# Last projection panel's context products beside the first neighbourhood jobs, and a layer norm's square sums joined ahead of the matrix engine

## The chip, the cores and the metric

The kernel runs on one core of a Trainium2 chip. The metric is the device time of one execution in microseconds (us); less is better. The core's engines work beside each other and wait for each other through semaphores: TensorE (PE, with its weight loads PEld), VectorE (DVE), ScalarE (ACT), GpSimd (POOL) and SyncE (SP), which here only issues transfers (DMAs). Each engine, and each DMA queue, works through its instructions in a fixed order.

## The reference

Two layers of a diffusion backbone over 512 latent tokens and 256 context tokens, width 1024, all in float32. What matters here:

```python
for l in range(DEPTH):                                   # 2 layers
    sh_a, sc_a, g_a, sh_f, sc_f, g_f = jnp.split(silu_c @ mod_w[l] + mod_b[l], 6, axis=-1)
    csh_a, csc_a, cg_a, csh_f, csc_f, cg_f = jnp.split(silu_cc @ mod_w[l] + mod_b[l], 6, axis=-1)
    a_lat = modulate(h_lat, sh_a, sc_a)                  # rms_norm(x) * (1 + scale) + shift
    a_ctx = modulate(h_ctx, csh_a, csc_a)
    # layer 0: p = a @ w_in; multi-head latent heads and 2-D neighbourhood heads; @ w_out
    # layer 1: sliding-window attention with grouped queries; @ w_out
    h_lat = h_lat + g_a * o_lat
    h_lat = h_lat + g_f * swiglu(modulate(h_lat, sh_f, sc_f), w_gate_up[l], w_down[l])
    # the context tokens likewise in layer 0
return rms_norm(h_lat, final_norm)
```

`rms_norm` divides each token by the root of the mean of its squared features. The six modulation vectors per layer and stream are products of a 1024-vector with a 1024 x 6144 matrix.

## The kernel before, in words

Features lie on the 128 partitions, tokens along the free dimension: a stream of width 1024 is eight tiles (k or m = 0 to 7) of 128 x 768, the first 512 columns latent (`LATS`), the last 256 context (`CTXS`). Every product is made of three matmuls of split operands (high by high, high by low, low by high; L319, L321 and L322 in `mm3`). A weight is loaded into `wr`, ScalarE casts it to a high part `wh` (L308), VectorE (or GpSimd) subtracts to a low part `wl` (L309). `wr`, `wh` and `wl` have three buffers each, the tiles `b` 24, `st` 12 and `p` 8. PSUM has three banks `s`, two `t`, two `d` and one `o`; `PG` takes the first seven in a ring, `PQ` always a `d`.

The order on each engine is made by a planner before the run: it simulates the program's instructions with a priority (by default the order in which the code emits them) and places on each engine what is ready first; `shifted(n)` lowers the priority by n. `behind(x, y)` orders x after y on an engine.

Layer 0 begins with the input projections. `projections()` is a generator of 96 steps: twelve panels of 128 columns, each with the latent half (four steps of two k) and the context half (four steps). The last two panels, 7 and 8 in `AFTER`, are queries and keys of neighbourhood pair 3. Beside the steps `bg` runs the generator `all_mods`: modulation components 2, 4 and 3 of layer 0, each as eight `mod_tile`s for two vectors, so 48 units; a unit is two VectorE instructions over half a weight row each (L237, 128 x 512), and at m = 7 one that adds the bias (L241). `PACE` tells how many units run beside each panel; before they sum to 48.

Then `attend(na_jobs())` runs four pairs of neighbourhood heads, three jobs each (context queries, latent queries 0 and 1, latent queries 2 and 3). A job's front is scores (L731, L732), softmax minimum on VectorE (L541), exponential on ScalarE (L537); its back is transposes (L484), copies (L475, L476) and value products (L530), one job later. Every fourth score tile lies in `wr`, the others in `p`. Between the parts `step` runs work of a first-in first-out list of side work at lower priority: `split_pair` (L1062 to L1071: splits for pairs 2 and 3, with copies through SP's queue), the latent heads' preparation and others. `STEPS[0]` is the number of such steps per job for each pair, `BG` the number of `bg` units per job. The bias tiles of the pairs are loaded by `nb_tiles` into `nb` and `b`. The multi-head latent heads follow (scores L1172).

At the end of layer 0, `output` makes the last part of the down projection for the latent and then the context stream, adds the residual (L1274) and feeds the norm of layer 1. Its latent square sums (`two=LATS`) are kept in three tiles: k = 0 to 3 on GpSimd, 4 and 5, and 6 and 7 on VectorE (L357 squares, L360 adds). `rstd` then sums over the partitions with one-column matmuls (L371, for each tile and each block of 128 tokens), takes the root (L374) and reciprocal (L375) and spreads it over the partitions (L351, a bank `o`). In the context stream, at group m = `SUMS[0]` the sums are made, and group `SUMS[1]` stands behind the spread. The norm's modulated tiles (`modulate`: L406 on VectorE, L407 on ScalarE, L408 on VectorE) go into the first products of layer 1 (L741 to L743).

Of the kernel before, what the change touches and what calls it, by code (L numbers as in the profile page):

```python
# [12 lines left out]
ALU = mybir.AluOpType  # L13

P = 128
D = 1024
KT = D // P
# [36 lines left out]
E1, EF = 1, 1  # L54
ORDER = ("2", "n3", "m", "")
AFTER = "012k5r678"
PACE = (3, 3, 3, 3, 5, 5, 5, 6, 5, 5, 3, 2)
KC = (1, 1, 0)
VP = 0
PT = (("p", "p", "p", "wr"), ("p", "p", "p", "wr"), ("p",))  # L60
# [4 lines left out]
LOWER = 150  # L65
LOE = {(0, 2, 0): None, (0, 2, 1): None, (0, 5, 0): None, (0, 5, 1): 1, (1, 2, 0): None, (1, 2, 1): None, (1, 5, 0): None, (1, 5, 1): None}
PATTERN = ("fbsfbsfbbsfs",) * 3
BG = (0, 0, 0, 0, 0)
LATE = ((0, 1, 3, 5, 7), ()), (0,) * 4 + (1, 2, 2, 2, 1, 2, 2, 2, 1, 2, 3, 2, 1, 2, 3, 2, 0, 0), ((2,), (2,)) + ((0, 2, 4, 6),) * 3
FIRST = 2000  # L70
SUMS = 5, 6
STEPS = ((2, 3, 4, 4), 5, 3)
HALVES = (slice(0, 256), slice(256, 512))
SWAP8 = [(i // 16) * 16 + (i % 16 + 8) % 16 for i in range(32)]
SWAP16 = [(i + 16) % 32 for i in range(32)]
# [23 lines left out]
def hybrid_kernel(ctx: ExitStack, tc, I, out):  # L99
# [6 lines left out]
    def T(tag, shape, dt=F32):  # L106
        count[0] += 1
        if tag not in SIZES:
            return sb.tile(shape, dt, tag=tag, name=f"{tag}_{count[0]}", bufs=BUFS.get(tag, 1))
        n = int(np.prod(shape[1:]))  # L110
        t = sb.tile([P, SIZES[tag] // (2 if dt == mybir.dt.bfloat16 else 4)], dt, tag=tag, name=f"{tag}_{count[0]}",
                    bufs=BUFS[tag])[: shape[0], :n]
        if len(shape) == 3:
            t = t.rearrange("p (a b) -> p a b", a=shape[1])
        return t
# [10 lines left out]
    def PG():  # L126

        ring[0] += 1
        return PS("stsdtsd"[ring[0] % 7])

    V, S, G, PE = nc.vector, nc.scalar, nc.gpsimd, nc.tensor

    def dma(o, i, eng=None):
        return (eng or nc.sync).dma_start(f(o), f(i))
# [4 lines left out]
    silu, marks = [], {}  # L139

    def behind(ins, *before):

        for x in before:
            tc.add_manual_dep(ins.ins, x.ins.name, mybir.DependencyInfo(mybir.DependencyClass.NoSync,
                              mybir.DependencyReason.DATA), reason="products in one run")
        return ins
# [22 lines left out]
    cond = T("cond", [P, 2, D])  # L169
# [20 lines left out]

    MOD, picks, started = {}, [], []

    dense = [True]

    def mods_pe(l, comp, get):

# [29 lines left out]
    def mod_tile(l, comp, m, vecs):  # L226

        at, one, ws = l * 48 + comp * 8 + m, float(comp in (1, 4)), []
        for i in range(2):
            ws.append(T(("ph", "pl")[i], [P, 512]))  # L230
            dma(ws[i], I["mod_w"][at, :, 512 * i : 512 * i + 512])
        for v in vecs:
            if m == 0:
                MOD[l, comp, v] = T(f"mod{l}{comp}{v}", [P, 8])
            t = MOD[l, comp, v]
            for i, w in enumerate(ws):
                behind(V.tensor_tensor_reduce(out=T("p", [P, 512], mybir.dt.bfloat16), in0=w, in1=cond[:, v, 512 * i : 512 * i + 512],  # L237
                                              op0=ALU.mult, op1=ALU.add, scale=1.0, scalar=t[:, m : m + 1] if i else 0.0,
                                              accum_out=t[:, m : m + 1]), *started)
            if m == KT - 1:  # L240
                V.scalar_tensor_tensor(t, t, one, modb[:, at - m : at + 1], op0=ALU.add, op1=ALU.add)  # L241
                for k in range(KT):
                    MOD[l, comp, v, k] = t[:, k : k + 1]
            yield
# [80 lines left out]
    def banks(cols, get, rows=P):  # L325

        return [(get()[:rows, : c.stop - c.start], c) for c in cols]

    def PQ():
        return PS("d")  # L330
# [22 lines left out]
    def square_sum(acc, src, c, tag="p", eng=None):  # L353

        n = c.stop - c.start
        t = B(tag=tag)
        marks["square"] = S.activation(t[:, :n], src[:, c], AF.Square)  # L357
        if acc is None:
            return t
        marks["add"] = (eng or V).tensor_tensor(acc[:, :n], acc[:, :n], t[:, :n], op=ALU.add)  # L360
        return acc
# [48 lines left out]
    class Norm:  # L410
# [6 lines left out]
        def add(self, k, c):  # L417
            if c is self.two:
                self.acc = self.acc if k else [None] * 3
                i = (k > 3) + (k > 5)  # L420
                self.acc[i] = square_sum(self.acc[i], self.src[k], c, eng=(G, V)[min(i, 1)])
            else:
                self.acc = square_sum(self.acc if k else None, self.src[k], c, eng=self.eng if k < KT - 1 else None)

# [297 lines left out]
    def put(t, rows=P, scale=1.0):  # L722
        def use(src, c):
            marks["put"] = S.activation(t[:rows, c], src, AF.Copy, scale=scale)

        return use
# [18 lines left out]
    def project(src, use, cols=(LATS, CTXS), m=P, every=2, eng=None, w=None, get=PQ):  # L745

        w = w or load_w(src, KT, m, eng)
        for c in cols:
            o, _ = banks([c], get, m)[0]
            for k in range(KT):  # L750
                mm3([(o, c)], (w[0][:, k : k + 1], w[1][:, k : k + 1]), A[k : k + 1], k == 0, k == KT - 1)
                if k % every == every - 1:
                    yield
            use(o, c)
# [141 lines left out]
    for k in range(KT):  # L896
        i = int(k > 5)
# [3 lines left out]
    diag, root = first_norm(accs, LATS, 0)  # L901
    scale = chunk(1, 0)
# [12 lines left out]
    for c in range(4):  # L915
# [16 lines left out]
        if c == 3:  # L932
            diag, _ = first_norm([acc], CTXS)
# [31 lines left out]
    def beside(gen):  # L965
        side_work.append(gen)
        return gen
# [66 lines left out]
    raws = []  # L1034

    def projections():

        for p in range(2):
            yield from project(I["w_in0"][p], put_q(sets[p][0], 0.125), get=PG)
            yield from project(I["w_in0"][p + 4], put_k(sets[p][1], KC[0]), get=PG)  # L1040
        for x in AFTER:
            if x in "012":
                lat_raw[int(x)] = B()
                yield from project(I["w_in0"][8 + int(x)], put(lat_raw[int(x)]), get=PG)
            elif x == "r":
                latent_roots()
            elif x == "k":
                kr.append(B())
                yield from project_narrow(I["w_kr"], put_rope(kr[0], rope0, SWAP8, 32, tag="p"))
            else:  # L1050
                raws.append(B(tag="p"))
                i = int(x) - 5
                yield from project(I["w_in0"][(2, 6, 3, 7)[i]], put(raws[i], scale=(0.125, 1.0)[i % 2]), get=PG)

    def split_pair(p):

# [153 lines left out]
                step()  # L1210
            ON.append(po)

    for i, _ in enumerate(projections()):
        n, r = PACE[i // 8], i % 8
        bg((r + 1) * n // 8 - r * n // 8)
    dense[0] = False
    attend(na_jobs())
    drain()

# [82 lines left out]
    def output(src, mov, l, comp, streams, norm, units, dst=None, keep=False, base=None, wait=0, held=()):  # L1302

        rest, kept, done = iter(()), [], []
        for i, (c, v) in enumerate(streams):
            late = i and norm.two
            before = done[-1:] + ([marks["add"]] if i and norm.two else [])
            for m in range(KT):
                w = kept[m] if keep and i else keep(src, m) if callable(keep) else load_w(src(m), len(mov), P, LOE[l, comp, i], "b" if keep else None, held[m : m + 1] * 2 if i == 0 else ())
                if keep and i == 0:  # L1310
                    kept.append(w)
                if late and m == SUMS[0]:
                    norm.hold = ins,
                    next(rest)
                    norm.hold, own = (), norm.marks[streams[0][0].start]
                    before = before + [own["diag"]]
                o = banks([c], PG)
                ins = mm3(o, w, mov)
                if m == 2 and i == 0 and (l, comp) == (0, 2):
                    behind(ins, marks["value"])  # L1320
                if late and m in SUMS:
                    behind(ins, own[("sum", "spread")[SUMS.index(m)]])
                done.append(behind(add_residual(m, o[0][0], l, comp, v, c, dst and dst[m], base and base(m, c)), *before))
                if c is TOK1:
                    G.dma_start(home[m], H[m])
                norm.add(m, c)
                if late and m >= SUMS[0]:
                    behind(marks["square"], own["root"])
                if m >= (SUMS[0] if late else wait):
                    next(rest, None)  # L1330
                if m in units[i]:
                    late_step(done[-1], m < 7)
            for _ in rest:
                pass
            rest = norm.rest(norm.acc, c, v)
        for _ in rest:
            pass
# [90 lines left out]
    norm, ops, sums = combined(H, 0, 3, TOK1, TOK2)  # L1428
# [260 lines left out]
    norm, ops, sums = combined(H, 1, 3, *HALVES)  # L1689
# [178 lines left out]
```

## Time and profile before

| | |
|---|---|
| median of 3 runs | 1553.22 us (1551.68 to 1554.38) |
| profiled execution | 1556.14 us, span of the core 1554.4 us |
| mean granted TensorE clock in it | 0.995 |
| PE / PEld / DVE / ACT / POOL busy, us | 1524.9 / 1373.6 / 1182.5 / 760.7 / 195.4 |
| moved by DMA | 225.95 MB, mean 145 GB/s |

A busy TensorE is not TensorE at its peak, since the ends of matmuls are modelled. In rows in order of time the first number is the start in us from the span's start, the second the duration; in brackets stands the idle time before and what ended it. Rows of waits give total us, times, longest. The granted clock is the share of full speed at which TensorE ran.

### The profile page before, as it was taken

The page shows a single profiled execution, that of the slowest core. Times are in us where ns is not written, and L with a number is a line of the kernel's source. Part 1 is how long each engine was busy: PE and PEld are TensorE (multiplying, and loading weights), DVE is VectorE, ACT ScalarE, POOL GpSimd, SP SyncE. Part 2 cuts the span into 40 slices and gives each one's busy share as a digit, 9 for nine tenths or more (in the row PEclk, how much of TensorE's full clock was granted, in tenths as well). Part 3 has the DMA queues.
Part 4 walks back from the last instruction along what each step waited for, and adds up shares of the span by engine and source line. Part 5 has one row for each costly group of instructions (what it writes and reads, how often), then busy time and mean ns, then how long its engine had stood idle before and what let it go on. Part 6 is the DMA issues. An engine that isn't in the chain of part 4 may idle for free.

```text
span 1554.4 us, 26610 instructions
## 1 busy us (share of the span) xinstructions
PE 1524.9 (98%) x10032; PEld 1373.6 (88%) x10032; DVE 1182.5 (76%) x2420; ACT 760.7 (49%) x1523; POOL 195.4 (13%) x266
## 2 busy tenths in 40 slices
PE   9999899999999999999999999999999999999998
PEld 8788787878999898999989998877889899898997
DVE  4799987776867686867768667789867779678685
ACT  4533676673555242433424335557846455354453
POOL 0022211000111102012021122560011000000001
PEclk9999999999999999999999999999999999999999
DMA  9675654244643636547375493200224224324322
GB/s 322 245 223 182 161 143 102 57 132 135 216 136 120 232 102 219 174 146 286 117 258 183 165 341 128 68 28 1 96 81 138 82 72 137 105 76 135 89 90 88
DMA packets 80931, 225.95 MB, mean 145 GB/s; under 512 B 11233, under 2 KB 18401, under 8 KB 80801
## 3 DMA queue, kind: packets, MB, share of 16 engines
q1 hardware_dynamic: 61968, 148.73, 30.3%
q0 software_dynamic: 17680, 73.94, 13.8%
q8 instruction: 79, 1.29, 0.3%
q10 hardware_dynamic: 1152, 1.57, 0.3%
q14 instruction: 52, 0.42, 0.1%
HBM read 186.97 MB, written 23.07 MB: 135 GB/s over the span
## 4 chain that ended last, share of the span: by engine, by line
PE 75%; DVE 8%; ACT 2%; issue 2%; DMA 2%; POOL 0%; DVEq 0%; ACTq 0%; POOLq 0%
PE pss L1439 5%; PE pso L530 5%; PE pss L1438 5%; PE pss L1437 5%; PE psd L319 3%; PE psd L321 3%; PE psd L322 3%; PE pss L319 3%; PE pss L322 3%; PE pss L321 3%; PE pst L1439 3%; PE pst L1437 3%; PE pst L1438 3%; PE pst L319 2%; PE pst L321 2%; PE pst L322 2%
## 5 line engine op out<-in xcount | busy, mean ns | idle before, releaser
L308 ACT CAST wh<-wr 128x1024 fp32r<-128x1024 f32 (+2 forms) x147 | 115.1, 798 | 224.1 <-DMA wr<-in_w_dn_dram 44.6
L309 DVE TENSOR_TENSOR wl<-wr,wh 128x1024 fp32r<-128x1024 f32 (+2 forms) x144 | 130.3, 912 | 87.4 <-ACT wh L308 83.2
L537 ACT ACTIVATE p<-p,sm 128x512 f32<-128x512 f32 (+3 forms) x144 | 105.1, 731 | 30.7 <-DVE sm L541 30.1
L1437 PE MATMUL pss<-b,wh 128*128 128x384 f32 (+1 forms) x346 | 107.6, 312 | 0.5 <-ACT b L345 0.5
L1438 PE MATMUL pss<-b,wh 128*128 128x384 f32 (+1 forms) x346 | 107.8, 312 | 0.1
L1439 PE MATMUL pss<-b,wl 128*128 128x384 f32 (+1 forms) x346 | 107.1, 311 | 0.4 <-DVE wl L1425 0.4
L321 PE MATMUL psd<-b,wh 128*128 128x512 f32 (+2 forms) x254 | 88.7, 349 | 0.0
L273 DVE CUSTOM_DVE_ANT_0 p<-rope,cond 128x1024 bf16<-128x1024 f32 x64 | 76.9, 1219 | 12.3 <-DMA rope<-in_mod_w_dram 12.2
L319 PE MATMUL psd<-b,wh 128*128 128x512 f32 (+2 forms) x214 | 78.7, 368 | 0.9 <-ACT wh L308 0.3
L322 PE MATMUL psd<-b,wl 128*128 128x512 f32 (+2 forms) x214 | 77.6, 363 | 0.0
L263 POOL DMA_DIRECT2D rope<-in_mod_w_dram x48 | 25.6, 534 | 411.6 <-DVE mod L273 390.9
L530 PE MATMUL pso<-ph,b 128*64 128x256 f32 (+1 forms) x400 | 77.0, 351 | 0.4 <-DVE ph L475 0.2
L530 PE MATMUL pso<-pl,b 128*64 128x256 f32 (+1 forms) x400 | 77.2, 351 | 0.0
L1439 PE MATMUL pst<-b,wl 128*128 128x384 f32 (+1 forms) x226 | 70.7, 313 | 1.0 <-DVE wl L1425 1.0
L1437 PE MATMUL pst<-b,wh 128*128 128x384 f32 (+1 forms) x226 | 70.6, 313 | 0.6 <-ACT p L1487 0.6
L1438 PE MATMUL pst<-b,wh 128*128 128x384 f32 (+1 forms) x226 | 70.5, 312 | 0.0
L1424 ACT CAST wh<-pl 128x512 fp32r<-128x512 f32 x78 | 45.0, 619 | 51.1 <-PE pss L1438 22.5
L1424 ACT CAST wh<-wr 128x1024 fp32r<-128x1024 f32 x39 | 41.0, 1052 | 56.8 <-PE pst L1438 14.8
L319 PE MATMUL pss<-st,wh 128*128 128x512 f32 (+2 forms) x198 | 67.6, 341 | 0.3 <-ACT wh L308 0.3
L322 PE MATMUL pss<-st,wl 128*128 128x512 f32 (+2 forms) x198 | 67.6, 341 | 0.1
L321 PE MATMUL pss<-b,wh 128*128 128x256 f32 (+2 forms) x208 | 66.0, 317 | 0.0
L1437 PEld LDWEIGHTS pss<-b,wh 128*128 128x128 f32 x346 | 65.0, 188 | 1.1 <-ACT b L345 0.8
(627 smaller groups left out, 5256.8 us busy)
## 6 DMA issues: line engine op xcount, KB each, us to landing
wr<-in_w_gu_dram SPq DMA_DIRECT2D x88, 512.0 KB, 4.0
rope<-in_mod_w_dram POOLq DMA_DIRECT2D x48, 512.0 KB, 3.9
wr<-in_w_dn_dram SPq DMA_DIRECT2D x73, 256.0 KB, 2.8
wr<-in_w_out_dram SPq DMA_DIRECT2D x32, 512.0 KB, 4.0
p<-home POOLq DMA_DIRECT2D x40, 384.0 KB, 5.6
home<-p POOLq DMA_DIRECT2D x40, 384.0 KB, 5.3
wr<-in_w_in_dram SPq DMA_DIRECT2D x21, 512.0 KB, 4.0
ph<-in_mod_w_dram SPq DMA_DIRECT2D x24, 256.0 KB, 3.0
```

Source lines behind the costliest of these rows:

```text
L273: behind(V.tensor_tensor_reduce(out=T("p", [P, D], mybir.dt.bfloat16), in0=w, in1=cond[:, v, :], op0=ALU.mult, op1=ALU.add, scale=1.0, sca ...
L308: behind(S.copy(h, r), *after[:1])
L309: behind((G if eng else V).tensor_tensor(lo, r, f(h), op=ALU.subtract), *after[1:])
L319: ins = PE.matmul(o, wh[:, k], mh[:, c], start=first and k == 0, stop=False)
L321: PE.matmul(o, wh[:, k], ml[:, c], start=False, stop=False)
L322: PE.matmul(o, wl[:, k], mh[:, c], start=False, stop=last and k == n - 1)
L530: ins = PE.matmul(o[64 * i : 64 * i + 64, c], v(kt), t, start=n == 0, stop=n == len(moving[i]) - 1)
L537: S.activation(p[:, c], p[:, c], AF.Exp, bias=nm, scale=-1.0, accum_out=dn)
L1424: S.copy(h, t)
L1437: PE.matmul(o, wh, xh, start=first and k == 0, stop=False, skip_group_check=not first)
L1438: PE.matmul(o, wh, xl, start=False, stop=False, skip_group_check=not first)
L1439: PE.matmul(o, wl, xh, start=False, stop=k == 3, skip_group_check=not first)
```

## The change

Three parts. First, only 92 of the 96 steps of `projections()` run before the neighbourhood jobs. The rest, the evacuation of the last panel's latent half and its 24 context products, becomes the first side work beside them (with a bank `d`); pair 0 has four side steps per job instead of two. Second, `PACE` runs 42 units beside the projections; the last six (component 3, m = 5, 6 and 7) run in the jobs of pairs 1 to 3, one unit per job. There a unit is one whole-row instruction (128 x 1024), the row is loaded into `wr`, the first by a unit of its own and the next when the last vector of a row is at hand. Third, in layer 1's norm two VectorE adds join the three latent square sums into one before `rstd`, the sums stand at context group 6 instead of 5 and the spread ahead of group 7, and the context stream's squares of groups 0 to 5 are emitted after the sums, behind the root on ScalarE.

```diff
-PACE = (3, 3, 3, 3, 5, 5, 5, 6, 5, 5, 3, 2)
+PACE = (3, 3, 3, 3, 5, 5, 5, 6, 5, 4, 0, 0)
...
-BG = (0, 0, 0, 0, 0)
+BG = (0, 1, 1, 1, 0)
...
-SUMS = 5, 6
-STEPS = ((2, 3, 4, 4), 5, 3)
+SUMS = 6, 7
+STEPS = ((4, 3, 4, 4), 5, 3)
...
-    dense = [True]
+    dense, early = [True], []
...
-        for i in range(2):
-            ws.append(T(("ph", "pl")[i], [P, 512]))
-            dma(ws[i], I["mod_w"][at, :, 512 * i : 512 * i + 512])
+        width = 512 if dense[0] else D
+
+        def whole(at):
+            w = T("wr", [P, D])
+            dma(w, I["mod_w"][at])
+            early.append(w)
+
+        if dense[0]:
+            for i in range(2):
+                ws.append(T(("ph", "pl")[i], [P, 512]))
+                dma(ws[i], I["mod_w"][at, :, 512 * i : 512 * i + 512])
+        else:
+            if not early:
+                whole(at)
+                yield
+            ws.append(early.pop())
         for v in vecs:
...
+            if not dense[0] and v == vecs[-1] and m < KT - 1:
+                whole(at + 1)
             for i, w in enumerate(ws):
...
                 self.acc[i] = square_sum(self.acc[i], self.src[k], c, eng=(G, V)[min(i, 1)])
+                if k == KT - 1:
+                    n, (a, b, d) = c.stop - c.start, self.acc
+                    for x in (d, a):
+                        marks["add"] = V.tensor_tensor(b[:, :n], b[:, :n], x[:, :n], op=ALU.add)
+                    self.acc = b
...
-                yield from project(..., get=PG)
+                yield from project(..., get=lambda: PG() if dense[0] else PQ())
...
-    for i, _ in enumerate(projections()):
+    panels = projections()
+    for i in range(92):
+        next(panels)
         n, r = PACE[i // 8], i % 8
         bg((r + 1) * n // 8 - r * n // 8)
     dense[0] = False
+    beside(panels)
     attend(na_jobs())
...
                     before = before + [own["diag"]]
+                    for j in range(m):
+                        norm.add(j, c)
+                        behind(marks["square"], own["root"])
...
-                norm.add(m, c)
+                if not late or m >= SUMS[0]:
+                    norm.add(m, c)
```

More of the change, by code (lines that the diff above doesn't have):

```diff
@@ L235, in mod_tile @@
             t = MOD[l, comp, v]
+            if not dense[0] and v == vecs[-1] and m < KT - 1:
+                whole(at + 1)
             for i, w in enumerate(ws):
-                behind(V.tensor_tensor_reduce(out=T("p", [P, 512], mybir.dt.bfloat16), in0=w, in1=cond[:, v, 512 * i : 512 * i + 512],
+                behind(V.tensor_tensor_reduce(out=T("p", [P, width], mybir.dt.bfloat16), in0=w,
+                                              in1=cond[:, v, width * i : width * i + width],
                                               op0=ALU.mult, op1=ALU.add, scale=1.0, scalar=t[:, m : m + 1] if i else 0.0,
@@ L1052, in projections @@
                 i = int(x) - 5
-                yield from project(I["w_in0"][(2, 6, 3, 7)[i]], put(raws[i], scale=(0.125, 1.0)[i % 2]), get=PG)
+                yield from project(I["w_in0"][(2, 6, 3, 7)[i]], put(raws[i], scale=(0.125, 1.0)[i % 2]),
+                                   get=lambda: PG() if dense[0] else PQ())
     def split_pair(p):
```

## The prediction

> **What bounds the kernel now.** I read the page first, then the granted clock by stretches, the order of time of each engine around the two places that the change touches, and last the waits of the same stretches.
>
> ```profile
> span 1554.4 us, 26610 instructions
> ...
> PE 1524.9 (98%) x10032; PEld 1373.6 (88%) x10032; DVE 1182.5 (76%) x2420; ACT 760.7 (49%) x1523; POOL 195.4 (13%) x266
> ...
> L273 DVE CUSTOM_DVE_ANT_0 p<-rope,cond 128x1024 bf16<-128x1024 f32 x64 | 76.9, 1219 | 12.3 <-DMA rope<-in_mod_w_dram 12.2
> ```
>
> TensorE is filled over the whole span, so time comes back only where it waits or runs slowly. The last line is the price of a modulation sum over a whole row: 1.22 us of VectorE.
>
> The largest hole of TensorE lies where the layer-0 projections end and the neighbourhood jobs begin. In order of time on TensorE:
>
> ```profile
> 163.42 0.28 PE L319 MATMUL pst<-b,wh 128*128 128x256 f32 x1
> ...
> 166.11 0.28 PE L322 MATMUL pst<-b,wl 128*128 128x256 f32 x1
> ...
> 167.06 0.28 PE L732 MATMUL pss<-st,st 128*128 128x256 f32 x1
> 171.57 0.58 PE L731 MATMUL pss<-st,st 128*128 128x256 f32 x1 [4.23 <-DVE sm L541]
> ```
>
> The 24 context products of the last panel fill 163.42 to 166.22 (0.117 us each), eight score products of the first job follow, and then TensorE stands for 4.23 us until the first softmax rows (L541). The stretch right behind (columns: stretch, its length, busy time of PE, PEld, DVE, ACT, POOL with counts, granted clock, DMA share, GB/s):
>
> ```profile
> 172.00:176.00 4.00, 4.00 (x20) 4.00 (x20) 3.12 (x11) 4.00 (x14) 0.58 (x1) 0.50 0.61 145
> ```
>
> So the hole costs twice: the granted clock falls to 0.50 behind it, and the matmuls of the first jobs run at half speed. On VectorE at the same time:
>
> ```profile
> 155.93 0.69 DVE L237 CUSTOM_DVE_ANT_0 p<-ph,cond 128x512 bf16<-128x512 f32 x1
> ...
> 167.33 0.75 DVE L237 CUSTOM_DVE_ANT_0 p<-pl,cond,mod 128x512 bf16<-128x512 f32 x1
> ...
> 168.13 2.18 DVE L241 SCALAR_TENSOR_TENSOR mod<-mod,modb 128x8 f32<-128x8 f32 x1
> 170.23 0.94 DVE L1064 TENSOR_TENSOR p<-p,b 128x768 fp32r<-128x768 f32 x1
> 171.09 0.41 DVE L541 CUSTOM_DVE_ANT_0 p<-pss,zeros 128x256 f32<-128x256 f32 x1
> ```
>
> VectorE is late because it is still adding modulation sums (L237): the last twelve halves run from 155.93 to 168.1, then the sum's bias (L241, stretched to 2.18 us) and the split of pair 2 (L1064). Scores were there by 166.5, their softmax began at 171.09.
>
> **The change, part by part.** *The last six modulation units* (m = 5, 6, 7 for two vectors, 12 half-row instructions) leave this place. Each pair took about 1.4 us, so 8.5 us of VectorE ahead of the first softmax go. Then VectorE is not the late one, and the end of the latent half of the last panel on TensorE is (163.42, unchanged: TensorE is full before it). Scores now follow there; the first L541 can run at about 163.9 instead of 171.09: **7.2 us earlier on VectorE**.
>
> *The 24 context products* move behind the first scores, with lower priority. They cost the same 2.8 us and lie in the time in which TensorE waits for softmax. TensorE's own account: 8 scores (0.96) and 24 products (2.80) from 163.42 end at 167.2, where 171.57 stood before: 4.4 us. The half speed from 171.57 to about 176.9 cost half of 5.3, 2.65 us, which also goes if no new hole of that kind opens. TensorE alone would give **7.0 us**.
>
> *What VectorE gets back.* Six whole-row sums at 1.22 us (7.3 us with nothing hidden), two in the jobs of pair 1, three in pair 2, one in pair 3, and the split L1064 (0.87 to its successor), which now stands behind the first softmax rows. The stretches of these jobs, same columns:
>
> ```profile
> 200.00:210.00 10.00, 9.92 (x85) 8.42 (x83) 10.00 (x26) 8.91 (x26) 2.21 (x4) 1.00 0.56 131
> 210.00:220.00 10.00, 10.00 (x81) 8.12 (x81) 6.33 (x20) 5.39 (x16) 0.28 (x1) 1.00 0.47 117
> 220.00:230.00 10.00, 10.00 (x87) 8.93 (x86) 9.22 (x24) 6.83 (x20) 2.44 (x4) 1.00 0.59 145
> 230.00:240.00 10.00, 9.38 (x72) 6.89 (x72) 4.64 (x9) 5.66 (x11) 4.29 (x4) 1.00 0.55 152
> ```
>
> From 210 to 240 VectorE is idle for 3.67 + 0.78 + 5.36 = 9.8 us: the four later sums (4.9 us) fit there, and I cost them at nothing; without that cover they cost 4.9. Up to 210 it is full, so the two sums of pair 1 and L1064 may cost 2.4 + 0.9 = 3.3 us: VectorE's lead would shrink from 7.2 to 3.9. But being full is not being late:
>
> ```profile
> PEld pss L731 <- DVE sm L541: 5.5, 5, 4.4
> ```
>
> Of five such waits between 150 and 250 us all but one are 1.1 us together; the rest is the hole itself. VectorE keeps up there, partly with work that can wait. So this part lies between −3.9 (VectorE pays in full) and −7.0 (TensorE alone). I take **−5.0**, nearer VectorE's end, since its row shows no room before 210.
>
> *Buffers and queues.* The input tiles of the projections are released product by product as the context half reads them; the second bias tiles of pair 0 wait for these buffers on SP's queue, and issue right after the first context product:
>
> ```profile
> 163.85 0.80 SPq L134 DMA_DIRECT2D b<-in_nb_dram  x2
> ```
>
> After the change that product comes about 1 us later, while softmax is 7 us earlier. The page of the stretch gives this load's landing:
>
> ```profile
> b<-in_nb_dram SPq DMA_DIRECT2D x4, 384.0 KB, 3.6
> ```
>
> So the tiles land at about 169; the first job's four 256-wide rows (0.41 each, above) and the second's four of twice the width (at most 0.82 each) keep VectorE from 163.9 until 168.8 at most. What is late next is this load: 0 to 2 us, inside the −5.0. The sums' fetches become three of 512 KB on SP instead of six halves, issued a job ahead into `wr`, which softmax also uses; I cost that at nothing as long as a `wr` buffer is free, a job (some 6 us) ahead of its use. Raising pair 0's side steps from 2 to 4 per job only makes room for the four panel steps; the split of pair 2 moves one job back, needed two pairs later: nothing.
>
> *Layer 1's norm.* TensorE, ScalarE and VectorE:
>
> ```profile
> 955.76 2.73 PE L371 MATMUL psd<-ones,p 128*128 128x1 f32 x24
> 958.35 0.40 PE L319 MATMUL pst<-st,st 128*128 128x256 f32 x1
> ...
> 963.55 0.50 PE L741 MATMUL pst<-b,wh 128*128 128x512 f32 x1 [0.83 <-ACT b L407]
> ```
> ```profile
> 956.08 1.98 ACT L357 ACTIVATE p<-b 128x256 f32<-128x256 f32 x5 [1.76 <-DVE b L1274]
> 958.08 1.28 ACT L374 ACT_TABLE_LOAD   x1
> 959.38 0.26 ACT L374 ACTIVATE sm<-psd,eps 128x4 f32<-128x4 f32 x1
> ```
> ```profile
> 953.51 2.08 DVE L360 TENSOR_TENSOR p<-p,p 128x512 f32<-128x512 f32 x2
> 955.51 0.47 DVE L1274 SCALAR_TENSOR_TENSOR b<-pss,mod,b 128x256 f32<-128x256 f32 x1
> ...
> 957.08 0.47 DVE L1274 SCALAR_TENSOR_TENSOR b<-pss,mod,b 128x256 f32<-128x256 f32 x1
> ...
> 959.67 0.18 DVE L375 RECIPROCAL sm<-sm 128x4 f32<-128x4 f32 x1 [2.12 <-ACT sm L374]
> ```
>
> Today 24 one-column matmuls take 2.59 us, context squares and a table load hold the root until 959.38, and the granted clock is half again (one microsecond; length, PE busy, clock, DMA share, GB/s):
>
> ```profile
> 959.00:960.00 1.00, 1.00 (x6) 0.50 1.04 385
> ```
>
> The change: two more 512-wide adds on VectorE (0.7 to 1.04 each by the L360 row; I take 0.7), one more context group (0.7) ahead of the sums, 8 instead of 24 sum instructions (0.86), and no context square before the root, so that the table load runs early. Adds end at 956.9, sums at 957.8, root at 958.1. The wait that replaces it: the reciprocal stands behind six context residuals (0.39 each: five begin from 955.51 to 957.08; now behind the adds), so about 959.3. The spread follows at 959.5, the first L741 about 2.2 us later (2.65 before, from a spread at half speed) at 961.7 instead of 963.55: **−1.8**. If the planner puts the reciprocal first, −2.9; if both adds take 1.04 and the postponed squares stand ahead of the first L407, +0.3. The squares of the context stream are needed only for products some 15 us later.
>
> **Sum.** 1556.14 (span 1554.4 and 1.74 around it) − 5.0 − 1.8 = **1549.3**. The profiled execution is 2.9 above the median of 1553.22 (runs 1551.68 to 1554.38), so this is 3.9 us, 0.25%, below the median. A measurement of this kernel tells about 0.2%, 3.1 us, from no change.
>
> The two half-speed stretches may not be in each run, which is why the profile may stand above the median. The Trainium skill, "TensorE: Matmul & The Clock Gate", section "Part 1: The HAM clock gate (the “warmup” mystery)", says that activity is judged in free-running windows of 3.4 us that don't start with the kernel; a hole then costs clock or not by where it falls. By that rule the gain against the median is the smaller one, 3.9 us, and the time stays 1549.3; were the stretches in each run, the whole 6.8 would come off the median: 1546.4, which is the second rival below.
>
> **Rivals.**
> 1. *VectorE gives it back.* The sums of pair 1 land in the full stretch, and the bias tiles are late: −2.5 instead of −5.0, and −1.2 in layer 1. 1552.4. For: VectorE 10.00 of 10. Against: 1.1 us of waits.
> 2. *The hole and its clock are in all runs*, so that the gain comes off the median: 1546.4. For: a wait of 4.23 is in the program's order. Against: the profile lies 1.8 above the slowest run.
> 3. *Slower: the fetch a job ahead isn't ahead.* SP's queue is in order. If a fetch finds no `wr` buffer, it waits for a softmax tile for about a job (6 us), the pair splits' copies behind it too, and VectorE stands at the sum with all later rows behind it. Three fetches: one such wait of 6 gives 1555.3, two give 1561; slower by 0.2% from 7.1 us of waits. Against: three `wr` buffers, one used per latent job.
> 4. *The planner leaves the context products late,* so that the hole stays (no scores or rows to fill it) and only VectorE's backlog moves: −1 and −1: 1554.
>
> **How the numbers follow.** Forecast 0.50, rival 1 0.20, rival 2 0.13, rival 3 with two waits 0.10, rival 4 0.07. Faster by over 0.2% (below 1550.1): four fifths of the forecast, whose own range is 1546.5 to 1551.5, and rival 2: 0.53. Slower (above 1556.3): rival 3, 0.10. Within: 0.37. The range 1545.8 to 1554.0 holds the forecast and rivals 1 and 2, reaches rival 4 and leaves out rival 3.
>
> **What would show it.** Right: no wait above 1.5 us on TensorE between 160 and 180 and a granted clock of 1.00 there; the first L541 near 164; the first L1172 scores of the latent heads 4 to 5 us earlier; 8 L371 sum instructions ahead of the first L741, and the way from the first context group (30 products ahead of 955.76) to it shorter by about 2 us. Wrong: waits of VectorE for `wr` from the modulation weights; waits of VectorE or ScalarE for the pair-0 bias tiles; TensorE waiting for L541 in the stretch of pairs 1 and 2; the reciprocal of layer 1 no earlier than before relative to the first context group.

## The result and the profile after

The change made the kernel slower by a little: 1557.32 us median (1551.12 to 1562.65), before 1554.48 (1551.68 to 1557.8), ratio 1.0017 [1.001, 1.0025], +2.6 us. The forecast was 1549.3. The profiled execution of after took 1556.88 us (span 1555.1, mean granted clock 0.993). Line numbers move: the sums L237 are now L252, the softmax rows L541 are L562, the scores L731 and L732 are L752 and L753, the sum matmuls L371 are L387, residuals L1274 are L1299, layer 1's first products L741 are L762, the latent heads' scores L1172 are L1194.

The head of the neighbourhood jobs came out as forecast. In order of time, VectorE of after (start, duration, in brackets the idle time before and what ended it):

```profile
162.99 0.43 DVE L562 CUSTOM_DVE_ANT_0 p<-pss,zeros 128x256 f32<-128x256 f32 x1 [7.49 <-PE pss L753]
```

VectorE now waits 7.49 us for the scores, where the scores had waited for it; the row comes 8.1 us earlier (0.6 of that is where the span begins). Then the lead is lost. The same three stretches, first of before, then of after (stretch, length, busy time of PE, PEld, DVE, ACT, POOL with counts, granted clock, DMA share, GB/s):

```profile
160.00:180.00 20.00, 15.77 (x94) 14.27 (x92) 17.95 (x44) 12.16 (x28) 7.23 (x7) 0.83 0.55 150
180.00:200.00 20.00, 19.92 (x170) 16.00 (x170) 19.19 (x50) 17.20 (x45) 2.15 (x4) 1.00 0.99 235
200.00:220.00 20.00, 19.92 (x165) 16.55 (x164) 16.33 (x45) 14.30 (x41) 2.50 (x4) 1.00 0.51 124
```
```profile
160.00:180.00 20.00, 18.63 (x143) 15.79 (x143) 12.92 (x36) 16.08 (x39) 5.42 (x6) 1.00 0.69 197
180.00:200.00 20.00, 17.65 (x130) 12.90 (x127) 19.61 (x46) 14.35 (x35) 2.15 (x4) 0.99 0.99 258
200.00:220.00 20.00, 19.98 (x158) 16.80 (x158) 18.07 (x52) 12.73 (x39) 2.50 (x4) 0.93 0.52 134
```

Up to 180 TensorE makes 143 matmuls instead of 94, at full clock. From 180 to 200 it makes 130 instead of 170: VectorE is full (19.61 of 20), and so are the DMA engines (0.99, as before). Where the moved sums ran, on VectorE of after:

```profile
179.54 1.22 DVE L252 CUSTOM_DVE_ANT_0 p<-wr,cond 128x1024 bf16<-128x1024 f32 x1 [1.08 <-DMA wr<-in_mod_w_dram]
...
188.93 1.22 DVE L252 CUSTOM_DVE_ANT_0 p<-wr,cond 128x1024 bf16<-128x1024 f32 x1
...
195.83 1.23 DVE L252 CUSTOM_DVE_ANT_0 p<-wr,cond 128x1024 bf16<-128x1024 f32 x1 [0.39 <-DMA wr<-in_mod_w_dram]
...
200.34 1.22 DVE L252 CUSTOM_DVE_ANT_0 p<-wr,cond 128x1024 bf16<-128x1024 f32 x1
...
208.56 1.22 DVE L252 CUSTOM_DVE_ANT_0 p<-wr,cond 128x1024 bf16<-128x1024 f32 x1
...
214.94 1.22 DVE L252 CUSTOM_DVE_ANT_0 p<-wr,cond 128x1024 bf16<-128x1024 f32 x1
```

Five of the six run before 210, ahead of the place where I had counted VectorE as idle (210 to 240), and two of them after a wait for their weight row. Who waits for whom from 165 to 245 us (total, times, longest):

```profile
PEld pss L752 <- DVE sm L562: 4.2, 9, 0.8
...
PE pss L752 <- DVE sm L562: 1.9, 4, 0.6
...
DVE p L252 <- DMA wr<-in_mod_w_dram: 1.5, 2, 1.1
```

The one wait of 4.23 us has become many small ones for the softmax rows, none over 0.8. The first score of the latent heads, before and after:

```profile
241.95 0.28 PE L1172 MATMUL pss<-st,st 96*128 96x256 f32 x1
```
```profile
240.27 0.38 PE L1194 MATMUL pss<-st,st 96*128 96x256 f32 x1
```

1.7 us earlier, 0.6 of it the span's start, instead of 4 to 5. Layer 1's norm, in order of time, TensorE, then ScalarE, then VectorE of after:

```profile
953.32 0.28 PE L335 MATMUL pst<-st,nb 128*128 128x256 f32 x1
...
958.33 1.05 PE L387 MATMUL psd<-ones,p 128*128 128x1 f32 x8 [0.54 <-DVE p L441]
```
```profile
955.49 1.28 ACT L390 ACT_TABLE_LOAD   x1
959.42 0.26 ACT L390 ACTIVATE sm<-psd,eps 128x4 f32<-128x4 f32 x1 [2.64 <-PE psd L387]
```
```profile
956.79 1.49 DVE L441 TENSOR_TENSOR p<-p,p 128x512 f32<-128x512 f32 x2
...
960.55 0.17 DVE L391 RECIPROCAL sm<-sm 128x4 f32<-128x4 f32 x1
```

Eight sum matmuls in 1.05 us, the table load hidden, the two joined adds at 0.7 each, the reciprocal last behind the residuals: the form that was forecast.

### The profile page after: what moved, and what is told of

Its sections match the earlier page's. It is cut to its first block, busy times and chain, and to the rows that moved or that the text cites. A ratio compares the mean times of both kernels' runs of the same rounds, so it can differ in the third digit from the quotient of the medians.

```text
span 1555.1 us, 26556 instructions
## 1 busy us (share of the span) xinstructions
PE 1527.1 (98%) x10016; PEld 1372.4 (88%) x10016; DVE 1180.0 (76%) x2410; ACT 761.6 (49%) x1523; POOL 194.4 (13%) x266
## 4 chain that ended last, share of the span: by engine, by line
PE 85%; DVE 7%; DMA 3%; ACT 2%; issue 2%; DVEq 0%; SPq 0%; ACTq 0%
PE pso L551 5%; PE psd L335 4%; PE pss L335 4%; PE psd L337 4%; PE psd L338 4%; PE pss L337 4%; PE pss L338 4%; PE pss L1468 4%; PE pss L1466 4%; PE pss L1467 4%; PE psd L1468 3%; PE psd L1467 3%; PE psd L1466 3%; PE pst L1468 3%; PE pst L1466 3%; PE pst L1467 3%
## 5 line engine op out<-in xcount | busy, mean ns | idle before, releaser
L325 DVE TENSOR_TENSOR wl<-wr,wh 128x1024 fp32r<-128x1024 f32 (+2 forms) x144 | 134.4, 940 | 77.2 <-ACT wh L324 72.6
L337 PE MATMUL psd<-b,wh 128*128 128x512 f32 (+2 forms) x266 | 90.9, 342 | 0.0
L335 PE MATMUL psd<-b,wh 128*128 128x512 f32 (+2 forms) x226 | 80.8, 357 | 0.5 <-ACT pl L497 0.5
L1468 PE MATMUL pss<-b,wl 128*128 128x256 f32 (+1 forms) x258 | 79.3, 307 | 1.5 <-DVE wl L1454 1.5
L1466 PE MATMUL pss<-b,wh 128*128 128x256 f32 (+1 forms) x258 | 79.4, 308 | 0.6 <-ACT p L1516 0.6
L335 PE MATMUL pss<-st,wh 128*128 128x512 f32 (+2 forms) x231 | 78.6, 341 | 0.4 <-ACT wh L324 0.4
L1467 PE MATMUL pss<-b,wh 128*128 128x256 f32 (+1 forms) x258 | 79.0, 306 | 0.0
L338 PE MATMUL pss<-st,wl 128*128 128x512 f32 (+2 forms) x231 | 78.5, 340 | 0.0
L1466 PE MATMUL pst<-b,wh 128*128 128x384 f32 (+1 forms) x234 | 72.3, 309 | 0.5 <-ACT b L361 0.5
L1467 PE MATMUL pst<-b,wh 128*128 128x384 f32 (+1 forms) x234 | 72.1, 308 | 0.0
L337 PE MATMUL pss<-b,wh 128*128 128x256 f32 (+2 forms) x226 | 72.0, 320 | 0.0
L1466 PE MATMUL psd<-b,wh 128*128 128x384 f32 (+1 forms) x210 | 65.7, 313 | 0.0
```

Source lines behind the costliest of these rows:

```text
L325: behind((G if eng else V).tensor_tensor(lo, r, f(h), op=ALU.subtract), *after[1:])
L335: ins = PE.matmul(o, wh[:, k], mh[:, c], start=first and k == 0, stop=False)
L337: PE.matmul(o, wh[:, k], ml[:, c], start=False, stop=False)
L338: PE.matmul(o, wl[:, k], mh[:, c], start=False, stop=last and k == n - 1)
L1466: PE.matmul(o, wh, xh, start=first and k == 0, stop=False, skip_group_check=not first)
L1467: PE.matmul(o, wh, xl, start=False, stop=False, skip_group_check=not first)
```

## The experiments

Each ratio is to the kernel before, timed on the same chip; one thousandth is 1.55 us. "Beside the latent heads" means behind the neighbourhood pairs.

**The norm alone.** Before, with `SUMS = 6, 7`, the joined adds and the postponed context squares.

```diff
-SUMS = 5, 6
+SUMS = 6, 7
...
+                        marks["add"] = V.tensor_tensor(b[:, :n], b[:, :n], x[:, :n], op=ALU.add)
...
+                    for j in range(m):
+                        norm.add(j, c)
```

> Only layer 1's norm is changed; the neighbourhood stage is that of before. Theory N (the norm change is what costs: its one-column sums, wait for the joined adds and wait for the reciprocal leave TensorE's clock at half speed over the first layer-1 products): 1.5 to 3 us above before, and the way from the first context group of the down projection to the end of layer 1's first products is no shorter. Theory V (the cost lies in the neighbourhood jobs, where the moved sums fill VectorE): the norm alone saves 0.5 to 1.5 us, as the 10.2 us from the first context group to the first product instead of 11.4 say.

Measured: 1551.55 (1550.04 to 1553.26), ratio 0.9989 [0.998, 0.9998], −1.7 us. The norm's term was right.

**The change without the norm.**

```diff
-SUMS = 6, 7
+SUMS = 5, 6
...
-                        marks["add"] = V.tensor_tensor(b[:, :n], b[:, :n], x[:, :n], op=ALU.add)
...
-                    for j in range(m):
-                        norm.add(j, c)
```

> The change without its norm part. Theory V: 2 to 4 us above before, no better than the whole change; the first softmax row near 163, the 25th softmax row of the stage no earlier than before, VectorE and DMA full from 172 to 200. Theory N: at or below before, by 0 to 1 us.

Measured: 1557.62 (1555.27 to 1561.19), ratio 1.0027 [1.0017, 1.0037], +4.2 us. The loss comes with the two parts at the neighbourhood jobs and not with the norm.

**The context products alone.** All 48 units ahead of the jobs, norm as before.

```diff
-BG = (0, 1, 1, 1, 0)
+BG = (0, 0, 0, 0, 0)
...
+    bg(48)
     dense[0] = False
     beside(panels)
```

> Only the last panel's context products are moved beside the first jobs; all 48 modulation units stay ahead of the jobs. Theory V: VectorE's backlog still delays the first softmax row to about 171, but 2.8 us of products fill TensorE's hole, no sum lies in the jobs: 1 to 3 us below before. Rival theory P (the moved products hold the input tiles, so that the second bias tiles and pair splits come late): 1 us or more above before, with softmax waiting for bias tiles.

Measured: 1555.19 (1552.63 to 1557.25), ratio 1.0007 [0.9997, 1.0018]: no difference that can be told, so neither expectation came.

**The sums beside the latent heads.** The whole change but for where the six sums go.

```diff
-BG = (0, 1, 1, 1, 0)
+BG = (0, 0, 0, 0, 1)
```

> The whole change, with the last six modulation sums beside the latent heads instead of neighbourhood pairs 1 to 3. Theory V: VectorE has room there (75 of 100 us busy), so the head's 7 us are kept in good part: 3 to 5 us below the whole change, 1 to 3 below before. Theory P or N: within 1 us of the whole change, since what they blame is unchanged.

Measured: 1549.49 (1546.79 to 1554.23), ratio 0.9977 [0.9966, 0.9988], −3.6 us, 6.2 below the change. This version beats both kernels. Its three stretches:

```profile
160.00:180.00 20.00, 18.61 (x141) 15.80 (x141) 13.84 (x37) 16.12 (x39) 5.57 (x6) 1.00 0.70 186
180.00:200.00 20.00, 19.48 (x160) 15.67 (x154) 19.18 (x52) 16.44 (x46) 2.15 (x4) 1.00 0.91 215
200.00:220.00 20.00, 19.96 (x166) 16.81 (x167) 15.33 (x44) 13.50 (x38) 3.03 (x5) 1.00 0.56 134
```

The same head as after (141 matmuls up to 180), and 160 instead of 130 from 180 to 200. The first score of the latent heads comes at 236.76, 5.2 us earlier than before (0.2 of it the span's start): the lead that was forecast.

**The sums alone in pairs 1 to 3.** Before, with `PACE`, `BG` and the whole-row units of the change; panels and norm as before.

```diff
-PACE = (3, 3, 3, 3, 5, 5, 5, 6, 5, 5, 3, 2)
+PACE = (3, 3, 3, 3, 5, 5, 5, 6, 5, 4, 0, 0)
...
-BG = (0, 0, 0, 0, 0)
+BG = (0, 1, 1, 1, 0)
```

> The move of the last six modulation sums into the jobs of pairs 1 to 3 alone; the context products of the last panel and the norm as in the kernel before. Theory V (the moved sums lengthen VectorE's full stretch of pairs 0 and 1 and TensorE waits for softmax there): the first softmax row comes some 4 to 6 us earlier than before, the lead is gone by the second part of pair 1, and the time is 2 to 4 us above the kernel before. Rival P (the loss needs the context products beside the jobs, which hold tiles and fill TensorE's room): the time is 1 to 3 us below the kernel before, as the hole ahead of the first softmax row goes and nothing is added to TensorE's jobs.

Measured: 1557.46 (1553.57 to 1560.57), ratio 1.0019 [1.0008, 1.0029], +3.0 us. The sums lose by themselves; the context products aren't needed for it.

**The sums alone beside the latent heads.** The same with

```diff
-BG = (0, 1, 1, 1, 0)
+BG = (0, 0, 0, 0, 1)
```

> The last six modulation sums stand beside the multi-head latent heads instead of pairs 1 to 3; the context products of the last panel and the norm as in the kernel before. Theory V: VectorE has room there, so the gain of taking the sums away from the head of the neighbourhood jobs comes through without the other two parts: about 1551 to 1552, 2 to 3 us below the kernel before, the rest of the 4.4 us of the version with all three parts being the norm's 1.7. Rival P (the head's gain needs the context products moved too): within 1 us of the kernel before.

Measured: 1553.61 (1551.45 to 1555.35), ratio 0.9991 [0.9982, 1.0], −1.4 us, which the interval barely tells from none and which lies between the two theories.

**Shorter sums, same fetch.**

```diff
-out=T("p", [P, width], mybir.dt.bfloat16), in0=w,
+out=T("p", [P, width if dense[0] else 128], mybir.dt.bfloat16), in0=w[:, : width if dense[0] else 128],
```

> The whole change, but each of the six moved sums adds only 128 of its row's 1024 columns (7/8 of the last three rows' sums are left out); the rows are loaded whole and held as long as in the change. Theory V (VectorE's time): the sums take about 0.25 instead of 1.2 us, 5 to 6 us less on VectorE, and the time falls to about 1550 to 1551, at least 4 us below the change. Rival T (the fetch: VectorE and softmax wait for the loaded rows and their buffers, or the transfers slow others): the time stays within 2 us of the change, about 1556 to 1558.

Measured: 1559.87 (1550.74 to 1562.96), ratio 1.0021 [1.0006, 1.0036]. Theory V, which knew only VectorE's time, fell: 5.6 us of VectorE's work taken away bring nothing by themselves. The trace says what took their place, VectorE in order of time:

```profile
193.07 0.69 DVE L562 CUSTOM_DVE_ANT_0 p<-pss,b 128x512 f32<-128x512 f32 x1
193.69 0.09 DVE L562 DVE_READ_ACCUMULATOR2_ANT sm<- 128x1 f32 x1
199.22 0.29 DVE L252 CUSTOM_DVE_ANT_0 p<-wr,cond 128x128 bf16<-128x128 f32 x1 [5.45 <-DMA wr<-in_mod_w_dram]
```

With shorter sums VectorE is earlier at the third one and stands 5.45 us for its row, which SP issued at 189.98 (so 9.2 us on its way); TensorE waits 5.02 us for the VectorE instruction behind it, and its clock halves:

```profile
196.00:200.00 4.00, 0.00 (x0) 0.00 (x0) 0.78 (x3) 0.72 (x3) 0.00 (x0) 0.74 1.04 326
200.00:204.00 4.00, 3.74 (x17) 3.34 (x17) 4.00 (x12) 2.30 (x6) 0.00 (x0) 0.50 0.77 164
```

**Full sums, no fetch.**

```diff
-            w = T("wr", [P, D])
-            dma(w, I["mod_w"][at])
-            early.append(w)
+            early.append(cond[:, 1, :])
```

> The whole change, but the six moved sums, at full width, read a row that is already in SBUF instead of a loaded weight row (the last three weight rows are not loaded, so their sums are of other data): no fetch, no weight buffer held, VectorE's work unchanged. Theory V: the time stays within 2 us of the change, about 1556 to 1557. Rival T (fetch and buffers): it falls to about 1550 to 1551.

Measured: 1554.72 (1551.33 to 1558.23), ratio 1.0001 [0.9991, 1.0011], about 2.5 us below the change. Between the two theories: the fetch is a part of the loss, not the whole.

**Neither.** The last two edits together.

```diff
-            w = T("wr", [P, D])
-            dma(w, I["mod_w"][at])
-            early.append(w)
+            early.append(cond[:, 1, :])
...
-out=T("p", [P, width], mybir.dt.bfloat16), in0=w,
+out=T("p", [P, width if dense[0] else 128], mybir.dt.bfloat16), in0=w[:, : width if dense[0] else 128],
```

> The whole change, but each of the six moved sums adds 128 columns only, of a row already in SBUF: neither their time on VectorE nor their fetch is left (the last three rows' sums are left out but for 128 columns of other data). Theory B (the loss has two parts, VectorE's six times 1.2 us and the fetch of each row in a stretch in which the DMA engines are full, so that VectorE stands for a row; a kernel with only one of them taken away can show the other grown): the level of the version with the sums beside the latent heads, 3 to 5.5 us below the kernel before, and 3 us or more below the version without the fetch. Rival C (the loss comes from the order of the context products and the pair split, whatever the sums do): within 1.5 us of the kernel before.

Measured: 1548.71 (1546.67 to 1553.17), ratio 0.9964 [0.9951, 0.9977], −5.6 us. With the sums all but gone the change is worth 5.6 us, so the moved sums cost 8 us in all (1.0017 / 0.9964): nearly 6 for their time on VectorE (1.0001 / 0.9964, from the version without fetch), and some 2.5 for the rows that come late. By their intervals such differences are good to 2 or 3 us. Rival C fell. The one profile of this version is of its slowest execution (1553.17): VectorE stands there for 2.88 us at 177.76 until a late transfer, and the first score of the latent heads comes at 241.03, no earlier than in the change. So the 8 us are shown by the times; no profile shows where this version gains them.

**The sums from pair 2 on.** The place that the prediction took as free.

```diff
-BG = (0, 1, 1, 1, 0)
+BG = (0, 0, 1, 2, 0)
```

> The whole change, but the moved sums begin with pair 2 (one unit per job in pair 2, two per job in pair 3) instead of pair 1: the place that the prediction counted as free, where VectorE was idle for 9.8 us and the DMA share was 0.47 to 0.59. Theory B: nearly all sums come behind the full stretch, so 3 to 5 us below the kernel before, like the version with the sums beside the latent heads. Rival R (wherever the sums are emitted among the pairs, they cost VectorE's 1.2 us each): 0 to 3 us above the kernel before.

Measured: 1562.18 (1555.44 to 1565.53), ratio 1.0046 [1.0032, 1.006], +7.2 us: the miss of these experiments, since theory B expected a gain. SP, VectorE and TensorE of this version in order of time:

```profile
193.72 4.86 SPq L134 DMA_DIRECT2D st<-st  x2
198.74 0.47 SPq L134 DMA_DIRECT2D wr<-in_mod_w_dram  x1
```
```profile
203.62 1.23 DVE L252 CUSTOM_DVE_ANT_0 p<-wr,cond 128x1024 bf16<-128x1024 f32 x1 [6.13 <-DMA wr<-in_mod_w_dram]
```
```profile
205.51 0.48 PE L505 MATMUL pst<-ident_r,wr 128*128 128x128 f32 x1 [6.31 <-DVE pl L496]
```

The first row is fetched by the unit just ahead of its sum's. SP issues it at 198.74, behind copies of the pair split that wait for their data, and VectorE is already there. One wait of 6.13 us costs TensorE 6.31, and the granted clock is 0.50 for some 10 us behind it. What the sums themselves would cost in that place stays untested: the late row hides it.

**The fetch one unit earlier.** The next row at the first instead of the second sum of a row.

```diff
-            if not dense[0] and v == vecs[-1] and m < KT - 1:
+            if not dense[0] and v == vecs[0] and m < KT - 1:
```

> The whole change, but the next weight row is fetched one unit earlier (at the first instead of the second sum of a row), two jobs ahead of its use. Theory B, if the fetch's share of the loss is VectorE standing for the late row: 1 to 2.7 us below the change, so 0 to 2 us above the kernel before. Rival Q (it is the transfers' share of full DMA engines, or a weight buffer held from the score tiles, which an earlier fetch holds longer): no gain, 2.5 us or more above the kernel before.

Measured: 1553.2 (1550.63 to 1554.94), ratio 0.9992 [0.9983, 1.0001], about 4 us below the change and no worse than the version with no fetch at all. This points to a fetch that costs by coming late and not by its bytes. By this version the fetch's share of the 8 us is 3.9 and that of VectorE's time 4.3 (0.9992 / 0.9964). In its profile only the second row is issued earlier (177.03 instead of 189.25; the first at 171.93 instead of 170.98, the third at 202.86 instead of 201.77), and VectorE waits for none. From issue to landing (KB each, median us), in the change, then here:

```profile
wr<-in_mod_w_dram SPq DMA_DIRECT2D x3, 512.0 KB, 6.6
```
```profile
wr<-in_mod_w_dram SPq DMA_DIRECT2D x3, 512.0 KB, 4.1
```

**The change once more.**

> The change itself once more, another profiled execution of the same program. Theory B: VectorE again stands for one or more of the moved sums' weight rows in 175 to 200 us, from 1 to 5 us in total by how late the transfers land, and the first score of the latent heads comes 0 to 3 us earlier than before. If the half-clock stretches fall by chance, they stand at other places or in another number than at 199, 350 and 961 us; if they follow from this program's order alone, at the same three places.

One execution: 1553.77, with before at 1554.77 beside it. No wait of VectorE for a weight row this time, so theory B's 1 to 5 us were not there; the first score of the latent heads stands where it did (240.19), the first L562 7.2 us earlier than before. From 180 to 200 TensorE made 151 matmuls, where the first profile of the change had 130 and before 170: a part of the fall in the first profile belongs to that execution. Two stretches of the change, in the first profile and in this one:

```profile
350.00:354.00 4.00, 4.00 (x21) 2.67 (x21) 1.83 (x5) 0.01 (x1) 0.00 (x0) 0.61 0.70 245
...
964.00:968.00 4.00, 4.00 (x11) 2.70 (x10) 4.00 (x8) 2.37 (x4) 1.51 (x2) 0.56 0.01 2
```
```profile
350.00:354.00 4.00, 4.00 (x33) 2.63 (x33) 2.21 (x5) 0.59 (x1) 0.00 (x0) 1.00 0.62 238
...
964.00:968.00 4.00, 4.00 (x21) 3.31 (x20) 4.00 (x8) 1.81 (x4) 0.76 (x1) 1.00 0.01 2
```

The same program in the same places, at half clock in one execution and at full clock in the other.

## Why the prediction was wrong, point by point

*VectorE's give-back* is the step that failed. I bounded it at 3.3 us (two sums of pair 1 and the split L1064), took 2.0 of that in the sum (−5.0 instead of −7.0), and put the four later sums at nothing because VectorE is idle for 9.8 us from 210 to 240. Measured, the six sums cost 8 us, with their fetch. Two things were wrong. Three sums ran by 197.1, the fourth by 201.6 and the fifth by 209.8, earlier than I had placed the jobs that issue them; I read the idle time of a place where the work didn't go. And "being full is not being late" held only as long as nothing was added: VectorE 19.19 of 20 with TensorE at 19.92 is a balance, and of the 7.3 us that the six sums take on VectorE some 4 to 6 came back as time of the kernel (4.3 by one pair of versions, 5.8 by the other).

*The fetch at nothing* failed too: it cost 2.5 to 3.9 us. A lead of a job, some 6 us, had no margin against 6.6 us to land (4.6 in the second profile). The row that warns of it was in the trace of before, DMA share 0.99 from 180 to 200; the prediction weighed only the rows from 200 to 240 (0.47 to 0.59). Rival 3 named the right wait but the wrong reason in the change itself (rows 6.6 us on their way on full DMA engines, where SP waited 0.2 us for a `wr` tile) and too high a price: 1.5 us of waits in one profile, none in the other. Its own form, a fetch stuck in SP's order, showed in the version with the sums from pair 2.

*The head* was right: first softmax row at 162.99 (forecast 163.9), waits of TensorE of at most 0.6 us up to 180, clock 1.00, the bias tiles inside the 0 to 2 us. *TensorE alone* was right within the noise: −7.0 and −1.8 from the profile are −7.1 against the median of the 22 runs of before (1554.48, so the profile lies 1.7 above it and not 2.9, as I had from three runs); the version with hardly any sums measured −5.6, with an interval from −7.6 to −3.6. That the profile stood above the median for its half-speed stretches is not borne out: its granted clock of 0.995 is a loss of 7.8 us, and other executions of before lost 8.2 to 8.5 on average. *The norm* was right, −1.8 against −1.7: from the first context group to the first L762 the way took 10.16 us in the first profile (half clock from the spread on) and 9.68 in the second, 11.38 before. *Buffers of the panels*: nothing, as said.

*The rivals.* Rival 1 had the mechanism, VectorE giving it back, priced at 2.5 us where it took more than all; rival 2's ground, that the hole and its clock are in all runs, agrees with these averages and with the profile of the norm alone (granted clock 0.83 from 160 to 180, as before), but the sums took its gain; rival 4 didn't happen. I had no case in which the four later sums cost their full length, which gives 1549.3 + 4.9 = 1554.2, and with 2.5 to 3.9 for the late rows 1556.7 to 1558.1, about what was measured.

**What stays open.** Each version is planned anew, so differences between them aren't pure prices. The 4 us between the change and the earlier fetch do not show in full in the profiles (the latent heads' scores differ by 0.7). Part is the clock: one minus the mean granted clock, times the span, is 8.4 us on average over the 22 executions of the change, 5.8 over the 11 with the earlier fetch, 5.6 over the 8 with hardly any sums and 4.8 with the sums beside the latent heads; for the kernel before it is 8.2 to 8.5. So up to 2.6 of the earlier fetch's 4 us, and up to 3.4 of the 3.6 us by which the sums beside the latent heads beat the kernel before, are granted clock. It is at most that: the two profiles of the change differ by over 5 us in this measure and by 3.1 in time. Nor does all of the change's loss stand at the neighbourhood jobs: in the first profile it leads by 1.7 us at the first score of the latent heads and by 0.4 at the last (344.8, before 345.2), and is 1.2 behind at the context groups ahead of the norm (953.32, before 952.17). The half clock at 350 can be 1.7 of this; why the latent heads took 1.2 us longer isn't known. How late the rows were in the executions without a profile isn't known. Nor is it settled why the context products alone brought nothing, with a first softmax row 4.3 us earlier.

## What to carry to other kernels

Before work is moved to where an engine is idle, look at when the program will really issue it, and read the whole stretch from there: where two engines are both full they are in balance, and what is added can cost most of its length. A prefetch needs a lead above the landing time in that stretch, not its size at a free DMA; issuing rows earlier was worth as much here, within the noise, as removing the transfer. And take the moved work out entirely once: what the version without it gains is about the most that a placing of it can bring (−5.6 us here; the best placing that was tried had −3.6).

## What the runs showed of the hardware

A halved clock can follow a stretch in which TensorE was only partly idle. In after the clock is 0.50 from 199.5 to 202.9:

```profile
196.00:200.00 4.00, 2.50 (x14) 1.61 (x14) 4.00 (x8) 2.32 (x6) 0.00 (x0) 0.94 1.03 266
200.00:204.00 4.00, 4.00 (x21) 3.59 (x20) 4.00 (x12) 1.85 (x7) 0.00 (x0) 0.64 0.62 151
```

TensorE was busy for 2.50 of 4 us, and the clock fell behind it. The same two stretches in the second profile of the change:

```profile
196.00:200.00 4.00, 2.75 (x19) 2.06 (x18) 4.00 (x9) 2.80 (x8) 0.00 (x0) 1.00 1.01 256
200.00:204.00 4.00, 3.02 (x21) 2.29 (x19) 4.00 (x11) 1.85 (x7) 0.00 (x0) 1.00 0.96 234
```

Holes of like size (2.75 of 4 us busy), and a clock of 1.00 throughout. The Trainium skill, "TensorE: Matmul & The Clock Gate", section "Part 1: The HAM clock gate (the “warmup” mystery)", puts the fall behind an idle window of about 3.4 us that runs free of the kernel's start. A window that runs free agrees with the two profiles, in which the fall came once and once not; that the window must be idle as a whole does not agree with the 2.50 us of work in the row above. So small holes put close together can cost clock too, in some executions, and a version whose TensorE has fewer of them gains twice (8.4 us of clock lost in the change, 4.8 with the sums beside the latent heads).
